# RWKV scan of a two-layer backbone: the substitution issued with its preparation, the group norm later and in another scratch tile, and merged products

## The chip, the cores and the metric

The program runs on one core of a Trainium2 chip. The metric is device time in microseconds (us), the median of several executions. The kernel before took 4250.28 us (three runs, 4240.55 to 4259.92).

The engines have short names: PE is the matrix engine (PEld its weight loads), DVE the vector engine, ACT the scalar engine, POOL the GpSimd engine, and SP the engine whose queue issues the DMAs. Each works through its own list of instructions strictly in order; semaphores tie the lists together.

## The reference, cut to what matters

The model has two layers. Each mixes tokens by four head groups, projects the result with `w_out`, and runs a convolutional feed-forward part. The change lies in one of the groups, RWKV-7, a recurrence over 1280 tokens in each of two directions:

```python
def rwkv_scan(r, w, k, v, a, b, state):
    def step(s_mem, inp):
        rt, wt, kt, vt, at, bt = inp
        sa = jnp.einsum('bhvk,bhk->bhv', s_mem, at)
        s_new = s_mem * wt[:, :, None, :] + sa[..., None] * bt[:, :, None, :] + vt[..., None] * kt[:, :, None, :]
        return s_new, jnp.einsum('bhvk,bhk->bhv', s_new, rt)
...
h, h_c = bidirectional_scan(rwkv_scan, rwkv_scan, ctx_fw, ctx_bw, lat_fw, lat_bw, init)
out = lambda hh, bon, gg: gg * (head_group_norm(from_heads(hh), ng, nb) + from_heads(bon))
```

## The kernel before

**Steps.** The recurrence is cut into ten steps of 128 tokens per direction (both directions in one step, each as two chunks of 64). `rwkv` is a generator; each `yield` hands over to the caller. A step s has four parts:

- `rwkv_prep(s)` loads the step's tiles, makes decays and the scaled products `bk` and `ar` on ACT, DVE and POOL, multiplies them on PE into `G`, and cuts the 16-wide diagonal blocks out of `G` into `NB`.
- `rwkv_inverse(s)` is the substitution: a DVE transpose of `NB` into `LM` (line 555), a POOL copy into `XL`, and 30 small POOL products and sums that invert the triangular blocks. `LM` and `XL` have one buffer each.
- `rwkv_tail(s)` builds the full inverse `XT` from `XL` by three DVE transposes and five groups of small matmuls with ACT copies (`ZC`, `Q`, `XT`) between them.
- `rwkv_chain(s)` is the recurrence: four times (two chunks, two directions) a product with the state `SV`, a copy `U` (line 634), a product with `XT`, a copy `VSA`, and the new state, scaled by `rho` (lines 621 and 644).

In program order a step is: substitution of step s+1, chain of s, group norm where two output tiles have become complete (steps 6 to 9, and step 1 in layer 0), tail of s+1, preparation of s+2. The group norm writes its squares and its result into `gq`, which takes the buffer of `LM`, and stores it by a DMA into `yw` (line 679).

**What runs beside it.** The mLSTM group runs in the same stage: after every second of its pieces (19 in layer 0, 17 in layer 1) the scan is advanced by one step. Matmuls for the modulation vectors (line 993, weights `adaw`) are spread between them. When both are through, the `w_out` weights are loaded in 32 pieces through eight buffers (`wst`, line 1060) and split into two halves `wo` by ACT (line 1035) and DVE (line 1036). `mix_out` then loads the groups' outputs (`yt`, line 1158; `gt`, line 1161), transposes them on PE (line 1166), scales them (`yT`), writes `uh` and `ul` (lines 1177, 1178), and multiplies with `wo` (lines 1042 to 1044).

**What sets the order.** The program text gives priorities. A scheduler puts each engine's instructions into one fixed list when the kernel is built, by its own estimate of when their inputs and buffers are ready. A change in one place can therefore move instructions of unrelated parts in that list. The lists of both layers differ from before only in the stage of the scan and just behind it.

Of the kernel before, what the change touches and what calls it, by code (L numbers as in the profile page):

```python
# [429 lines left out]
def rwkv(K,l,pv,last,p1,p2,p3):  # L430


    nc=K.nc; tt=nc.vector.tensor_tensor
    YF=p1.tile([128,10,4,64],F32,name="YF")
    W2=p1.tile([128,512],F32,name="W2"); nc.gpsimd.memset(W2,0.0)
    for i,(w,o) in enumerate((('rwkv_w2','rwkv_w0'),('rwkv_a2','rwkv_a0'))):
        nc.sync.dma_start(W2[i*64:i*64+32].rearrange("p (d c) -> p d c",d=2),K.a[w][l].rearrange("d p c -> p d c"))
        nc.sync.dma_start(W2[i*64+32:i*64+33],K.a[o][l:l+1].rearrange("o d c -> o (d c)"))
    TWA=p1.tile([128,2,2,128],F32,name="TWA"); nc.gpsimd.memset(TWA,0.0)
    rmask=p1.tile([128,2,128],F32,name="rmask"); nc.sync.dma_start(rmask,K.a['c_rwmask'])  # L440
    xl0=p1.tile([128,32,8],F32,name="xl0"); nc.sync.dma_start(xl0,K.a['c_xl0'])
    smask=p1.tile([128,4*65],F32,name="smask"); nc.gpsimd.memset(smask,1.0); nc.gpsimd.memset(smask.rearrange("p (a b) -> p a b",b=65)[:,:,0:1],0.0)
    kas=p1.tile([128,2,2,2],F32,name="kas")
    for a in range(2):
        r=slice(64,128) if a==0 else slice(0,64); o=slice(0,64) if a==0 else slice(64,128)
        nc.gpsimd.memset(kas[o,a],-0.5)
        nc.vector.tensor_scalar(out=kas[r,a,0],in0=pv['ka'][r],scalar1=0.5,scalar2=None,op0=ALU.mult)
        nc.vector.tensor_scalar(out=kas[r,a,1],in0=pv['ka'][r],scalar1=-0.5,scalar2=1.0,op0=ALU.mult,op1=ALU.add)
    AR=[p1.tile([128,2,2,2,2,2,64],F32,name="AR%d"%i) for i in range(3)]
    for t in AR: nc.gpsimd.memset(t[64:128,:,:,:,0],0.0); nc.gpsimd.memset(t[0:64,:,:,:,1],0.0)  # L450
    XT=[p1.tile([128,2,4,128],F32,name="XT%d"%i) for i in range(2)]
    for t in XT: nc.gpsimd.memset(t,0.0)
    I32=p1.tile([128,32],F32,name="I32"); hm=p1.tile([128,2],F32,name="hm"); PI=p1.tile([128,2,4,32],F32,name="PI")
    for i in range(4): nc.scalar.activation(out=I32[i*32:i*32+32],in_=K.ident[i*32:i*32+32,i*32:i*32+32],func=ACTF.Copy)
    for i in range(2): nc.vector.tensor_reduce(out=hm[:,i:i+1],in_=I32[:,i*16:i*16+16],axis=XS,op=ALU.add)
    for i in range(2): nc.scalar.activation(out=PI[:,i],in_=I32.unsqueeze(1).to_broadcast([128,4,32]),func=ACTF.Copy)
    C=dict(AR=AR,XT=XT,I32=I32,hm=hm,PI=PI,YF=YF,W2=W2,TWA=TWA,rmask=rmask,xl0=xl0,smask=smask,kas=kas,p=p2,p3=p3,l=l,pv=pv,last=last,seen=set())
    NS=10
    st=[rwkv_prep(K,C,0)]
    rwkv_inverse(K,C,st[0]); rwkv_tail(K,C,st[0])  # L460
    st.append(rwkv_prep(K,C,1))
    for s in range(NS):
        yield
        if s+1<NS: rwkv_inverse(K,C,st[s+1])
        rwkv_chain(K,C,st[s],st[s+1] if s+1<NS else None,s)
        if s==1 and not last or s>5:
            a,b={1:(8,9),6:(3,4),7:(2,5),8:(1,6),9:(0,7)}[s]
            sl=slice(a,b+1,b-a)
            group_norm(K,YF[:,sl],K.D['yw'].rearrange("(t p) c -> p t c",p=128)[:,sl],2,p2.tile([128,1056],F32,tag="LM",name="gq")[:,0:512].rearrange("p (a t) -> p a t",t=64),"gnw")
        if s+1<NS: rwkv_tail(K,C,st[s+1])  # L470
        if s+2<NS: st.append(rwkv_prep(K,C,s+2))


def rwkv_prep(K,C,s):
# [41 lines left out]
    ar=C['AR'][s%len(C['AR'])]; bk=p3.tile([128,2,2,2,2,64],F32,tag="BK",name="bk")  # L516
    for a in range(2):
        for ft in range(2): act(out=bk[:,:,ft,:,a],in_=As[:,:,ft].rearrange("p d (c t) -> p d c t",t=64),func=ACTF.Identity,scale=C['kas'][:,a,0,ft:ft+1],bias=C['kas'][:,a,1,ft:ft+1])
        for d in range(2): tt(out=bk[:,d,:,:,a],in0=bk[:,d,:,:,a],in1=v4(rkk[:,d,4-2*a:6-2*a]),op=A.mult)
    G=p.tile([128,2,2,2,2,128],F32,tag="G",name="G",bufs=3); bt=p.tile([128,2,2,2,2,64],F32,tag="BKT",name="bt",bufs=3)  # L520
    NB=p.tile([128,2,4,32],F32,tag="NB",name="NB")
    for d in range(2):
        E,N=Ep[:,d],En[:,d]
        if d==0: Wp,W,Wi=E[:,:,:,0:64],E[:,:,:,1:65],N[:,:,:,1:65]
        else: Wp,W,Wi=N[:,:,:,1:65],N[:,:,:,0:64],E[:,:,:,0:64]
        for q in range(2):
            r=slice(q*64,q*64+64)
            (nc.gpsimd if d==0 else nc.vector).tensor_tensor(out=ar[r,d,:,:,q,0],in0=v4(rkk[r,d,6:8]),in1=Wp[r],op=A.mult)
            tt(out=ar[r,d,:,:,q,1],in0=v4(rkk[r,d,0:2]),in1=W[r],op=A.mult)
        for a in range(2): tt(out=bk[:,d,:,:,a],in0=bk[:,d,:,:,a],in1=Wi,op=A.mult)  # L530
        for c in range(2):
            b=bank()
            for f in range(2): mm(b[:,f*256:f*256+256],bk[:,d,f,c].rearrange("p a t -> p (a t)"),ar[:,d,f,c].rearrange("p q a t -> p (q a t)"),start=True,stop=True)
            tt(out=G[:,d,c].rearrange("p f q t -> p (f q) t"),in0=b.rearrange("p (a t) -> p a t",a=4),in1=C['rmask'][:,d].unsqueeze(1).to_broadcast([128,4,128]),op=A.mult)
        for q in range(2):
            for blk in range(2):
                r=slice(q*64+blk*32,q*64+blk*32+32)
                src=G[r,d,:,:,q,blk*32:blk*32+32].rearrange("p c f t -> p (c f) t")
                if d==0: nc.vector.transpose(out=NB[r,0],in_=src)
                else: act(out=NB[r,1],in_=src,func=ACTF.Copy)  # L540
        b=bank()
        for c in range(2):
            for f in range(2):
                nc.tensor.transpose(b[:,c*256+f*128:c*256+f*128+128],bk[:,d,f,c].rearrange("p a t -> p (a t)"),K.ident)
        act(out=bt[:,d].rearrange("p c f q e -> p (c f q e)"),in_=b,func=ACTF.Copy)
# [3 lines left out]
def rwkv_inverse(K,C,P):  # L549

    nc=K.nc; A=ALU; p=C['p']; NB=P['NB']
    LM=p.tile([128,1056],F32,tag="LM",name="LM"); LD=LM.rearrange("p (b s) -> p b s",b=2)
    X=P['X']=p.tile([128,384],F32,tag="XL",name="XL")
    XD=X.rearrange("p (b s) -> p b s",b=2)[:,:,0:64].rearrange("p b (i j) -> p b i j",j=4); tmp=X[:,256:376].rearrange("p (b i j) -> p b i j",b=2,j=4)
    nc.vector.transpose(out=LM[:,0:1024].rearrange("p (j i) -> p j i",i=32),in_=NB.rearrange("p d u j -> p j (d u)").unsqueeze(2).to_broadcast([128,32,4,8]))
    nc.gpsimd.tensor_copy(out=X[:,0:256].rearrange("p (h i j) -> p h i j",h=2,j=4),in_=C['xl0'].rearrange("p i (h j) -> p h i j",h=2))
    for j in range(15):
        n,m=15-j,j//4+1; t_=tmp[:,:,0:n,0:m]
        nc.gpsimd.tensor_tensor(out=t_,in0=LD[:,:,j*33+1:j*32+16].unsqueeze(3).to_broadcast([128,2,n,m]),in1=XD[:,:,j:j+1,0:m].to_broadcast([128,2,n,m]),op=A.mult)
        nc.gpsimd.tensor_tensor(out=XD[:,:,j+1:16,0:m],in0=XD[:,:,j+1:16,0:m],in1=t_,op=A.add)  # L560
# [53 lines left out]
def rwkv_chain(K,C,P,Pn,s):  # L614
# [3 lines left out]
    rho=p.tile([128,2,2,2],F32,tag="rho",name="rho",bufs=2)  # L618
    for i in range(2):
        if i and not Pn: break  # L620
        for d in range(2): tt(out=rho[:,i,d],in0=io[:,1,d,:,i^d],in1=(Pn if i else P)['io'][:,0,d,:,d if i else 1-d],op=A.mult)
    need_y=not(C['last'] and s<2); YF=C['YF']
    if need_y: y=K.ybank(); yb=[y[:,0:256],y[:,256:512]]
    for i in range(2):
# [40 lines left out]
def group_norm(K,Y,out_y,nt,sqt,tag="gn",pool=None):  # L665

    nc=K.nc
    v=Y[:,0:nt]; h=Y.shape[2]; n=nt*h; th=lambda t: t[:,:n].rearrange("p (t h) -> p t h",h=h)
    q=sqt[:,:n].rearrange("p (t h) d -> p t h d",h=h)
    s,r=[th((pool or K.p_sm).tile([128,n],F32,tag=tag,name="gn_"+i,bufs=2)) for i in "sr"]  # L670
    nc.vector.tensor_reduce(out=s,in_=v,axis=mybir.AxisListType.X,op=ALU.add)
    nc.vector.tensor_scalar(out=s,in0=s,scalar1=1.0/64,scalar2=None,op0=ALU.mult)
    nc.vector.tensor_tensor(out=v,in0=v,in1=s.unsqueeze(3).to_broadcast([128,nt,h,64]),op=ALU.subtract)
    nc.scalar.activation(out=q,in_=v,func=ACTF.Square)
    nc.vector.tensor_reduce(out=r,in_=q,axis=mybir.AxisListType.X,op=ALU.add)
    nc.scalar.activation(out=r,in_=r,func=ACTF.Sqrt,scale=1.0/64,bias=K.eps5)
    nc.vector.reciprocal(out=r,in_=r)
    (nc.gpsimd if nt==2 else nc.vector).tensor_tensor(out=q,in0=v,in1=r.unsqueeze(3).to_broadcast([128,nt,h,64]),op=ALU.mult)
    nc.sync.dma_start(out_y,q.rearrange("p t h d -> p t (h d)"))
# [789 lines left out]
```

## Time and profile before

| what | value |
|---|---|
| median of three runs | 4250.28 us |
| profiled execution | 4248.15 us, span 4246.4 us, granted clock 0.946 of full speed |
| PE busy in the span | 3951.2 us (93%) |
| DVE busy | 2537.2 us (60%) |
| scan stage, layer 0 | 767 to 1185 us of the span |
| scan stage, layer 1 | 2933 to 3360 us of the span |

The profile is of one execution; its rows are added up against its own 4248.15 us, which lies 2.1 us under the median. The stage is where step 0 of the scan begins until the last matmul of its last chain. "Idle before" in a row is the time for which the engine had nothing running, and behind the arrow stands what ended it.

### The profile page before, as it was taken

How to read it: one execution, taken by the hardware profiler on the slowest of the kernel's cores; microseconds unless marked ns; L12 is line 12 of the kernel's file. 1: busy time of each engine (PE TensorE's matmuls, PEld its weight loads, DVE VectorE, ACT ScalarE, POOL GpSimd, SP SyncE). 2: the span in 40 equal slices, each digit the busy share in tenths (PEclk: the TensorE clock that was granted, in tenths of full speed). 3: DMA queues.
4: the chain of work that ended last, by engine and by line, in shares of the span. 5: the costliest groups of instructions: out<-in, count | busy, mean ns of one | idle time of the engine just before them, and what ended most of it. 6: DMA issues, size and time to landing. Idle time of an engine off the chain costs nothing.

```text
span 4246.4 us, 70484 instructions
## 1 busy us (share of the span) xinstructions
PE 3951.2 (93%) x28176; PEld 3225.0 (76%) x28176; DVE 2537.2 (60%) x4756; ACT 1413.6 (33%) x2849; POOL 764.7 (18%) x1538
## 2 busy tenths in 40 slices
PE   5999999799979999999997999997899799999998
PEld 2788887677768888888885678886776678888886
DVE  5755665777669444444448565677767684444447
ACT  4433333554344211111113433344543442212121
POOL 3320023323312000000021221025432220000002
PEclk6999999799989999999998999998898799999999
DMA  4235554344443110111103325554333331111112
GB/s 165 76 96 180 151 156 121 109 149 125 129 147 120 46 40 30 45 40 35 35 30 121 90 87 157 171 162 118 118 115 109 124 111 55 50 40 55 45 50 99
DMA packets 477154, 414.50 MB, mean 98 GB/s; under 512 B 48827, under 2 KB 443284, under 8 KB 474010
## 3 DMA queue, kind: packets, MB, share of 16 engines
q1 hardware_dynamic: 476826, 409.99, 31.1%
q8 instruction: 222, 3.64, 0.3%
q14 instruction: 106, 0.87, 0.1%
HBM read 323.65 MB, written 86.25 MB: 97 GB/s over the span
## 4 chain that ended last, share of the span: by engine, by line
PE 53%; DVE 9%; DMA 4%; issue 2%; ACT 2%; POOL 1%; SPq 1%; DVEq 0%; ACTq 0%; POOLq 0%
PE bank L1043 9%; PE bank L1042 9%; PE bank L1044 9%; PE dbank L1042 6%; PE dbank L1043 6%; PE dbank L1044 6%; DVE bst L1003 1%; DMA xt<-x 1%; DVE facc L1225 1%; PE mbank L993 1%; PE bank L186 1%; DMA adaw<-in_ada_w 1%; PE bank L187 1%; DVE facc L1226 0%; DMA wst<-in_w_out 0%
## 5 line engine op out<-in xcount | busy, mean ns | idle before, releaser
L1042 PE MATMUL dbank<-uh,wh 128*128 128x512 f32 (+1 forms) x2120 | 763.7, 369 | 8.6 <-ACT tmpB L398 5.5
L1043 PE MATMUL dbank<-ul,wh 128*128 128x512 f32 (+1 forms) x2120 | 759.8, 367 | 0.0
L1036 DVE TENSOR_TENSOR wl<-wst,wh 128x1024 fp32r<-128x1024 f32 x146 | 185.9, 1275 | 510.3 <-ACT wh L1035 355.1
L1044 PE MATMUL dbank<-uh,wl 128*128 128x512 f32 (+1 forms) x2120 | 481.5, 367 | 0.0
L1042 PEld LDWEIGHTS dbank<-uh,wh 128*128 128x128 f32 x2120 | 400.6, 189 | 84.0 <-ACT tmpB L398 5.9
L1043 PEld LDWEIGHTS dbank<-ul,wh 128*128 128x128 f32 x2120 | 400.9, 189 | 68.7 <-issue 1.1
L1044 PEld LDWEIGHTS dbank<-uh,wl 128*128 128x128 f32 x2120 | 365.7, 188 | 71.0 <-issue 1.7
L1284 DVE TENSOR_TENSOR facc<-facc,bank 128x512 f32<-128x512 f32 x324 | 221.8, 687 | 205.1 <-PE bank L1044 205.1
L1042 PE MATMUL bank<-uh,wh 128*128 128x512 f32 (+1 forms) x920 | 334.9, 372 | 4.5 <-ACT uh L1030 4.5
L1043 PE MATMUL bank<-ul,wh 128*128 128x512 f32 (+1 forms) x920 | 335.1, 372 | 0.8 <-DVE ul L1031 0.8
L1042 PE MATMUL bank<-wdh,gh 128*128 128x512 f32 x792 | 315.6, 400 | 15.7 <-DVE facc L1298 5.7
L1043 PE MATMUL bank<-wdl,gh 128*128 128x512 f32 x792 | 310.4, 392 | 1.0 <-DVE wdl L1036 1.0
L1253 POOL MEMSET fz<- 128x1 f32 x132 | 7.3, 99 | 1433.4 <-DVE fc L1268 1213.5
L1044 PE MATMUL bank<-wdh,gl 128*128 128x512 f32 x792 | 247.7, 391 | 0.0
L1035 ACT ACTIVATE wh<-wst 128x1024 fp32r<-128x1024 f32 x146 | 154.7, 1060 | 237.5 <-PE dbank L1043 164.5
L1035 ACT ACTIVATE wdh<-wst 128x1024 fp32r<-128x1024 f32 x46 | 48.8, 1062 | 523.7 <-PE bank L1044 431.4
L1044 PE MATMUL bank<-uh,wl 128*128 128x512 f32 (+1 forms) x920 | 211.9, 372 | 0.0
L1042 PEld LDWEIGHTS bank<-uh,wh 128*128 128x128 f32 x920 | 174.1, 190 | 36.1 <-ACT uh L1030 5.6
L1043 PEld LDWEIGHTS bank<-ul,wh 128*128 128x128 f32 x920 | 174.2, 189 | 31.9 <-DVE ul L1031 1.7
L1042 PEld LDWEIGHTS bank<-wdh,gh 128*128 128x128 f32 x792 | 149.7, 189 | 56.9 <-DVE facc L1298 11.0
L1044 PEld LDWEIGHTS bank<-uh,wl 128*128 128x128 f32 x920 | 161.5, 188 | 33.1
L1043 PEld LDWEIGHTS bank<-wdl,gh 128*128 128x128 f32 x792 | 149.7, 189 | 34.6 <-issue 3.2
(490 smaller groups left out, 7856.9 us busy)
## 6 DMA issues: line engine op xcount, KB each, us to landing
wst<-in_ffn_w_up SPq DMA_DIRECT2D x88, 512.0 KB
adaw<-in_ada_w SPq DMA_DIRECT2D x160, 256.0 KB
wst<-in_w_in SPq DMA_DIRECT2D x58, 512.0 KB
wst<-in_ffn_w_down SPq DMA_DIRECT2D x46, 512.0 KB
df<-in_c_F SPq DMA_DIRECT2D x10, 1344.0 KB
xt<-x SPq DMA_DIRECT2D x26, 512.0 KB
df<-in_c_I SPq DMA_DIRECT2D x8, 1344.0 KB
rkk<-wrk SPq DMA_DIRECT2D x10, 1024.0 KB
```

The costliest lines, as they stand in the source:

```text
L186: mm(dst_re,F[:,i],pre(slot),start=True,stop=False); mm(dst_re,F[:,i+1],pim(slot),start=False,stop=True)
L187: mm(dst_im,F[:,i],qim(slot),start=True,stop=False); mm(dst_im,F[:,i+2],qre(slot),start=False,stop=True)
L993: for j in range(2): nc.tensor.matmul(ps[32*j:32*j+2,0:128],k.sc[:,q],w[u][q//2][:,q%2,j*128:j*128+128],start=(q==0),stop=(q==7))
L1003: for h in range(2): nc.vector.bn_stats(out=st[:,h],in_=x[h])
L1035: k.nc.scalar.activation(out=h,in_=st,func=ACTF.Copy)
L1036: k.nc.vector.tensor_tensor(out=lo,in0=st,in1=h,op=ALU.subtract)
L1042: mm(ps,lh,rh,start=(i==0),stop=False)
L1043: mm(ps,lh,rl,start=False,stop=False)
L1044: for i,((lh,ll),(rh,rl)) in enumerate(pairs): mm(ps,ll,rh,start=False,stop=(i==n-1 and more is None))
L1225: for o,i,gg in zip([y[:,h] for h in hs],x,[g[:,h] for h in hs]) if parts else [(y,x,g)]: stt(out=o,in0=i,scalar=m,in1=gg,op0=ALU.subtract ...
L1253: for q in (0,1025,1282): nc.gpsimd.memset(z[:,q:q+1],0.0)
L1284: else: tt(out=d,in0=d,in1=ps,op=ALU.add)
```

## The change

Three things are edited. The substitution of step s+2 is written directly behind that step's preparation, so in the program's order it stands one hand-over to the mLSTM earlier, and the group norm is written after tail, preparation and substitution. The group norm's scratch `gq` takes the buffer of `As` (an input of the preparation) and no longer that of `LM`. In the preparation, pairs of DVE products with 256 elements per partition become one with 512 (lines 519 and 530), and the products for `rho` move from DVE to POOL.

```diff
     st=[rwkv_prep(K,C,0)]
     rwkv_inverse(K,C,st[0]); rwkv_tail(K,C,st[0])
-    st.append(rwkv_prep(K,C,1))
+    st.append(rwkv_prep(K,C,1)); rwkv_inverse(K,C,st[1])
     for s in range(NS):
         yield
-        if s+1<NS: rwkv_inverse(K,C,st[s+1])
         rwkv_chain(K,C,st[s],st[s+1] if s+1<NS else None,s)
+        if s+1<NS: rwkv_tail(K,C,st[s+1])
+        if s+2<NS: st.append(rwkv_prep(K,C,s+2)); rwkv_inverse(K,C,st[s+2])
         if s==1 and not last or s>5:
             a,b={1:(8,9),6:(3,4),7:(2,5),8:(1,6),9:(0,7)}[s]
             sl=slice(a,b+1,b-a)
-            group_norm(K,YF[:,sl],K.D['yw'].rearrange("(t p) c -> p t c",p=128)[:,sl],2,p2.tile([128,1056],F32,tag="LM",name="gq")[:,0:512].rearrange("p (a t) -> p a t",t=64),"gnw")
-        if s+1<NS: rwkv_tail(K,C,st[s+1])
-        if s+2<NS: st.append(rwkv_prep(K,C,s+2))
+            group_norm(K,YF[:,sl],K.D['yw'].rearrange("(t p) c -> p t c",p=128)[:,sl],2,p3.tile([128,8,64],F32,tag="As",name="gq"),"gnw")
...
-        for d in range(2): tt(out=bk[:,d,:,:,a],in0=bk[:,d,:,:,a],in1=v4(rkk[:,d,4-2*a:6-2*a]),op=A.mult)
+        tt(out=bk[:,:,:,:,a].rearrange("p d f c t -> p d (f c) t"),in0=bk[:,:,:,:,a].rearrange("p d f c t -> p d (f c) t"),in1=rkk[:,:,4-2*a:6-2*a].rearrange("p d f (c t) -> p d (f c) t",t=64),op=A.mult)
...
-        for a in range(2): tt(out=bk[:,d,:,:,a],in0=bk[:,d,:,:,a],in1=Wi,op=A.mult)
+        bka=bk[:,d].rearrange("p f c a t -> p (f c) a t"); tt(out=bka,in0=bka,in1=Wi.rearrange("p f c t -> p (f c) t").unsqueeze(2).to_broadcast([128,4,2,64]),op=A.mult)
...
-        for d in range(2): tt(out=rho[:,i,d],in0=io[:,1,d,:,i^d],in1=(Pn if i else P)['io'][:,0,d,:,d if i else 1-d],op=A.mult)
+        for d in range(2): nc.gpsimd.tensor_tensor(out=rho[:,i,d],in0=io[:,1,d,:,i^d],in1=(Pn if i else P)['io'][:,0,d,:,d if i else 1-d],op=A.mult)
```

The scheduler's lists show three places where more than the edited lines moved. Line numbers of the changed kernel are one lower from line 472 on.

The first is DVE in layer 1, around the transpose `LM` of the last substitution (step 9). Before, with `gq` and `LM` in one buffer:

```order
L657 TENSOR_TENSOR YF<-ybank,YF 128x2x64 x4
L671 TENSOR_REDUCE gn_s<-YF 128x8
L579 SCALAR_TENSOR_TENSOR PI<-cbank,hm,I_25746 128x4x16 x2
L672 TENSOR_SCALAR gn_s<-gn_s 128x8
L673 TENSOR_TENSOR YF<-YF,gn_s 128x2x256
L675 TENSOR_REDUCE gn_r<-gq 128x8
```

The transpose stands eleven rows further down (line 555), behind this group norm of step 7. In the changed kernel:

```order
L554 STREAM_TRANSPOSE LM<-NB 128x1024
L643 TENSOR_TENSOR SV<-cbank,rho 64x128 x2
L670 TENSOR_REDUCE gn_s<-mV 128x8
L656 TENSOR_TENSOR YF<-ybank,YF 128x2x64 x4
L578 SCALAR_TENSOR_TENSOR PI<-cbank,hm,I_25706 128x4x16 x2
L671 TENSOR_SCALAR gn_s<-gn_s 128x8
L670 TENSOR_REDUCE gn_s<-YF 128x8
```

The transpose moved ahead of the group norm of step 7, and no longer waits for that norm's store.

The second is ACT at the end of the scan in layer 1, where the halves `wo` of `w_out` are made. Before, in the tail of step 9 (`ZC`, `XT`, `Q`):

```order
L637 ACTIVATE VSA<-cbank 64x128
L1035 ACTIVATE wo_31114<-wst 128x256 x4
L1035 ACTIVATE wo_31116<-wst 128x256 x4
L586 ACTIVATE ZC<-cbank 128x128
L1035 ACTIVATE wo_31118<-wst 128x256 x4
L591 ACTIVATE XT_25743<-cbank 32x8x32 x4
L1035 ACTIVATE wo_31120<-wst 128x256 x3
L599 ACTIVATE Q<-cbank 128x128
L1035 ACTIVATE wo_31120<-wst 128x256
```

In the changed kernel, in the chain of step 9 (`U`, `VSA`):

```order
L609 ACTIVATE XT_25703<-cbank 32x4x32
L633 ACTIVATE U<-cbank 128x128
L636 ACTIVATE VSA<-cbank 64x128
L633 ACTIVATE U<-cbank 128x128
L1034 ACTIVATE wo_31034<-wst 128x256 x4
L1034 ACTIVATE wo_31036<-wst 128x256 x4
L636 ACTIVATE VSA<-cbank 64x128
L1034 ACTIVATE wo_31038<-wst 128x256 x3
L633 ACTIVATE U<-cbank 128x128
L1034 ACTIVATE wo_31038<-wst 128x256
```

All 32 splits moved from the tail of step 9 and the first half of the last chain to behind the second `U` of that chain.

The third is SP behind the scan of layer 1, with the loads `yt` for the first transposes of `mix_out`. Before:

```order
L1158 DMA yt<-yr_110 128x2x256
L1158 DMA yt<-yw_111 128x2x256
L679 DMA ym_108<-gq 128x2x256
L1060 DMA wst<-in_w_out 128x256 x22
L679 DMA yw_111<-gq 128x2x256
L1060 DMA wst<-in_w_out 128x256 x2
L679 DMA yw_111<-gq 128x2x256
L1212 DMA rg<-in_ln_g 128x1024
```

In the changed kernel:

```order
L1059 DMA wst<-in_w_out 128x256 x24
L1211 DMA rg<-in_ln_g 128x1024
L1211 DMA rb<-in_ln_b 128x1024
L1183 DMA xt<-x_116 128x1024 x2
L678 DMA yw_111<-gq 128x2x256
L1157 DMA yt<-ym_108 128x2x256
L1157 DMA yt<-yh_109 128x2x256
L1157 DMA yt<-yr_110 128x2x256
L1157 DMA yt<-yw_111 128x2x256
```

The first `yt` loads moved behind all `w_out` loads and the scan's last store `yw`; the 20 transposes that read them and stood on PE before the last tail's end now stand behind the last chain.

## Rows read from the trace of the kernel before

**Rows 1.** Windows, 767 to 1185 and 2933 to 3360 together: length, busy us of each engine.
```profile
sum 845.00, PE 732.92 PEld 570.00 DVE 602.07 ACT 396.49 POOL 282.02; mean PE 366.46 PEld 285.00 DVE 301.03 ACT 198.25 POOL 141.01
```
**Rows 2.** PE's waits, layer 0, 847 to 1185: us in total, times, longest.
```profile
PE mbank L993 <- DVE NUM L805: 2.0, 1, 2.0
...
PE cbank L585 <- DVE PI L579: 0.4, 1, 0.4
```
**Rows 3.** PE's waits, layer 1, 3014 to 3360.
```profile
PE cbank L605 <- ACT Q L599: 7.6, 3, 6.1
...
PE mbank L961 <- DVE ab L960: 3.5, 3, 2.2
...
PE cbank L585 <- DVE PI L579: 0.7, 1, 0.7
```
**Rows 4.** DVE by source line: count, ns shortest/median/longest, first to last start, forms.
```profile
L519 DVE TENSOR_TENSOR bk<-bk,rkk x80: 379/418/1260, 781.1 to 3230.7; 128x256 f32<-128x256 f32 x80
...
L530 DVE TENSOR_TENSOR bk<-bk,Ep x40: 385/422/1148, 784.5 to 3233.1; 128x256 f32<-128x256 f32 x40
...
L621 DVE TENSOR_TENSOR rho<-io x76: 143/152/991, 787.4 to 3295.1; 128x2 f32<-128x2 f32 x76
...
L1174 DVE TENSOR_TENSOR yT<-yT,gt x27: 671/684/693, 1208.0 to 3435.6; 128x512 f32<-128x512 f32 x27
```
**Rows 5.** POOL's smallest product, 767 to 3390: busy us, mean ns.
```profile
L559 POOL TENSOR_TENSOR XL<-LM,XL 128x8 f32<-128x8 f32 x20 | 4.4, 222 | 1.6
```
**Rows 6.** Timeline: start, us, engine; two DVE products beside one POOL product.
```profile
3230.39 1.59 DVE L519 TENSOR_TENSOR bk<-bk,rkk 128x256 f32<-128x256 f32 x2
...
3230.51 1.19 POOL L778 TENSOR_TENSOR mRU<-mVO,cmbd 8x512 f32<-8x512 f32 x1 [4.81 <-PE mbank L781]
```
**Rows 7.** Source line 555, what ended DVE's idle time; then two rows of PE's timeline.
```profile
  DMA yw<-gq: 6.4, 4
...
3309.74 0.66 PE L635 MATMUL cbank<-U,XT 128*128 128x64 f32 x4 [2.85 <-ACT XT L610]
...
3314.49 2.82 PE L1166 MATMUL dbank<-ident,yt 128*128 128x128 f32 x12
```
**Rows 8.** Timeline, tail of step 9: layer 0, then layer 1.
```profile
1150.63 0.68 DVE L569 STREAM_TRANSPOSE T<-XL 128x128 f32<-128x128 f32 x2
...
1166.40 0.27 ACT L610 ACTIVATE XT<-cbank 32x128 f32<-32x128 f32 x1
...
3323.61 0.69 DVE L569 STREAM_TRANSPOSE T<-XL 128x128 f32<-128x128 f32 x2
...
3343.09 0.27 ACT L610 ACTIVATE XT<-cbank 32x128 f32<-32x128 f32 x1
```
**Rows 9.** Timeline of ACT, layer 1: splits of `w_out` and the last chain.
```profile
3328.06 2.56 ACT L1035 ACTIVATE wo<-wst 128x256 fp32r<-128x256 f32 x8 [2.55 <-DMA ym<-gq]
...
3334.99 0.42 ACT L1035 ACTIVATE wo<-wst 128x256 fp32r<-128x256 f32 x1 [2.39 <-DMA wst<-in_w_out]
...
3342.20 0.26 ACT L634 ACTIVATE U<-cbank 128x128 f32<-128x128 f32 x1
...
3346.27 0.28 ACT L634 ACTIVATE U<-cbank 128x128 f32<-128x128 f32 x1
3347.55 0.76 ACT L1035 ACTIVATE wo<-wst 128x256 fp32r<-128x256 f32 x2 [1.00 <-DMA wst<-in_w_out]
```
**Rows 10.** Timeline, layer 1: the scan's last store, the first product of `mix_out`.
```profile
3365.73 0.38 SPq L679 DMA_DIRECT2D yw<-gq  x1
...
3369.09 0.80 PE L1042 MATMUL bank<-wo,uh 128*128 128x512 f32 x1 [4.26 <-ACT uh L1177]
```
**Rows 11.** Timeline, transposes behind the first `yt` loads, layer 0; scaling and split, layer 1.
```profile
1212.29 1.09 PE L1166 MATMUL dbank<-ident,yt 128*128 128x128 f32 x4 [2.90 <-DMA yt<-ym]
...
3377.34 1.94 ACT L1169 ACTIVATE yT<-dbank,pvm 128x256 f32<-128x256 f32 x4 [2.51 <-POOL ul L1178]
3379.30 1.06 ACT L1177 ACTIVATE uh<-yT 128x1024 fp32r<-128x1024 f32 x1
```

## The prediction

> **What bounds the kernel now.** I read five views in this order: the page, busy time by windows, PE's waits in the two scan stages, DVE's instructions by source line, and the timelines of steps 8 and 9 of the scan with what follows them.
>
> Outside the scan's stages, and the first products behind them, nothing is touched. Inside them PE works 732.9 of 845 us [rows 1]. The change adds and removes no matmul, so even an ideal result could only take from the other 112 us, about 56 per layer. DVE works 602 us of the same 845 and POOL 282 [rows 1]: neither is full, and POOL has the most room.
>
> What PE waits for is read next, from step 2 of the scan on. In layer 0 it waits for DVE on seven lines, from `NUM` with 2.0 us to `PI` with 0.4, together 6.0 us [rows 2]. In layer 1 the first line of all is the copy `Q` of ACT, 7.6 us, of which 6.1 is one wait; DVE is behind six lines, from `ab` with 3.5 to `PI` with 0.7, together 9.5 us [rows 3]. So PE loses 15.5 us to DVE in both layers, and no line names POOL. The substitution, which the change moves, is thus not waited for directly in the middle of the scan. It is waited for at one place in an indirect way: the transpose `LM` sits idle 6.4 us in four cases until the group norm's store has read `gq` out of the same buffer, and behind it PE waits 2.85 us for an `XT` at 3309.74 [rows 7].
>
> **The change part by part.**
>
> *Merged products.* Per step, four pairs of 128x256 products on DVE become four products of 128x512. A product takes 0.418 us (line 519) or 0.422 (line 530), and a 128x512 product of two f32 inputs elsewhere in the kernel 0.684 [rows 4]. A pair saves 2×0.42−0.684 = 0.156 us; 80 pairs in 20 steps save 12.5 us of DVE.
>
> *`rho` to POOL.* 76 products of 0.152 us leave DVE [rows 4]: 11.6 us. POOL's nearest product, 128x8, takes 0.222 us [rows 5], so POOL gets 76×0.222 = 16.9 us, over both stages, on top of 282. In POOL's list they stand behind the substitution that feeds the same step's tail, and so in front of the next one. I cost them at nothing: they need only the decays of two preparations, and the state product that reads them comes a whole tail later. If that cover is gone, all 16.9 us would be late; at best they cost nothing.
>
> *What DVE's relief is worth.* DVE loses 24.1 us of work, 1.2 per step, 4% of its 602. What PE can gain from it is bounded by 0 and by 24.1, if DVE set every step. Of the 15.5 us that PE waits for DVE, 9.2 are for the mLSTM and the modulation (`NUM`, `ab`, `modc`, `S` and the like), which wait for their own chains, and 6.3 for products of the scan. I take half of the scan's 6.3, since half of such a chain's length is copies and transposes that stay: −3 us. Of step 0, whose preparation nothing covers, I count the four pairs in full: 4×0.156×2 layers = −1.2 us.
>
> *Another buffer for `gq`, and the substitution earlier.* The transpose `LM` no longer stands behind the norm's store. The bounds are 0 and the 6.4 us of [rows 7]; I take the one wait that PE saw, −2.9 us. What is late next there is the copy chain of the tail itself. `As`, the new buffer, is an input of a preparation, so the next preparation could wait for the store in its turn; it comes half a step later, and in the last four steps, where the norm runs, there are hardly any preparations left (the last is that of step 9). I cost that at nothing; its upper bound is the same 6.4 us.
>
> *The end of layer 1.* Here the lists move most, though no line of it was edited.
> The 20 transposes of `mix_out` that stood between steps 8 and 9 on PE leave that place. Twelve of them took 2.82 us [rows 7]; all 20 would be 4.7 at that rate. Between 2.8 and 4.7 I take −3.7.
> The tail of step 9 loses its neighbours, the splits of `w_out` on ACT. In layer 1 it lasts from 3323.61 to 3343.36, 19.75 us; in layer 0, where no split stands in it, from 1150.63 to 1166.67, 16.04 [rows 8]. I take the difference, −3.7; the bounds are 0 and −7.6, all of `Q`'s waits [rows 3].
> The last chain pays for it. Now it lasts 17.8 us, from its first `U` at 3342.20 to the end of the stage at 3360.0. The splits took ACT from 3328.06 to 3348.3, 20.3 us with their waits for loads, the longest 2.39 [rows 9]. In the changed list all 32 come behind the second `U`, which is 4.1 us into the chain, and the chain's copies stand between them. The chain then lasts 4.1+20.3 = 24.4 us: +6.6. At best ACT's copies slip through at no cost (0); at worst each of the six copies that follow waits for another late load, 6×2.39 = 14.3 more than the 6.6.
> The loads `yt` now stand behind the last store `yw`. That was issued at 3365.73, 5.7 us behind the stage's end, and the first product of `mix_out` began at 3369.09, 9.1 us behind it [rows 10]. With the loads behind the store, what layer 0 and the later tiles show comes in a row: 2.9 us for the load, 1.09 for four transposes, 1.94 for the scaling, 1.06 for `uh` [rows 11]. 5.7+2.9+1.1+1.9+1.1 = 12.7: +3.6. Bounds 0 (modulation products fill the gap) and +7.
>
> *The sum.* −3 −1.2 −2.9 −3.7 −3.7 +6.6 +3.6 = −4.3 us. The profiled execution took 4248.15 us, so 4243.9; the median of the runs is 2.1 higher, so the forecast is 4246 us.
>
> **A rule against the rows.** In [rows 6] two DVE products of line 519 took 1.59 us together, where two of the median are 0.84; a POOL product of 1.19 us began 0.12 us behind the start of the first. The longest of that line is 1.26 us, three times the median [rows 4]. So POOL's work can hold DVE's. The Trainium skill, "SBUF — State Buffer", section "SBUF: two separate sides", says that the two engines share a pair of ports that one of them locks for its whole instruction, a DVE operation with two inputs from SBUF against a POOL operation that reads SBUF. The trace agrees (1.59 us in place of 0.84). By that rule `rho` on POOL would relieve DVE by less than is counted above, which the third rival prices from rows.
>
> **The rivals.**
>
> *First: DVE sets the steps.* PE's waits name many small releasers, and an engine at 71% that feeds each hop of a chain may delay every hop. Then the whole relief of 24.1 us (step 0's included) falls on the path: −24.1 −2.9 −3.7 −3.7 +6.6 +3.6 = −24.2, so 4226 us. Against it: only 15.5 us of PE's waits end on DVE at all [rows 2, 3], and a good part of DVE's work is done for the mLSTM, which gains nothing here.
>
> *Second, on the slower side: the hand-over to `mix_out` in layer 1.* Place: the last chain on ACT, and SP's queue in front of `yt`. The splits wait for loads that come through eight buffers, and a copy of the chain that stands behind a split waits with it. If each of the six copies behind the second `U` meets a load 2.39 us late [rows 9], the chain lasts 14.3 us more, PE has nothing else there, and if the steps and the tail save nothing the sum is −1.2 −3.7 +6.6 +14.3 +3.6 = +19.6: 4270 us. It decides from the point where eight pieces are not loaded when the second `U` is done. For it: three splits already waited 1.0 to 2.55 us for transfers [rows 9]. Against it: the loads need nothing of the scan and have all of tail 9 to fill the eight buffers.
>
> *Third: POOL holds DVE.* If each `rho` on POOL holds DVE for its 0.222 us, 16.9 of the 24.1 us come back, and 7.2 stay. The gain in the steps falls from 3 to 0.9: 4248 us.
>
> *Fourth: it does not do what it says.* The substitution could stand where it stood, since the scheduler orders lists by its own estimate. The lists say otherwise for step 9; in the middle of the scan PE waits for no substitution, so the move is worth nothing there, which the sum already has.
>
> **How the numbers follow.** What a measurement of this kernel can tell from no change is about 0.5%, 21 us: faster means under 4229, slower over 4271.5. The forecast has a chance of 0.58, the first rival 0.17, the second 0.15, the third 0.10. The forecast's own range takes the bounds of its terms partly together: from −12 (6.4 instead of 2.9, chain at no cost) to +8 (the chain at 14.3 with the tail saved), 4236 to 4258. The range that should hold the time takes in the first rival and most of the second's way: 4225 to 4266. Faster: the first rival and a little of the forecast's lower end, 0.20. Slower: the part of the second rival over 4271, and terms that I have not seen, 0.13. The rest, 0.67, is no change.
>
> **What would show it.** Line 518's and 529's products as 128x512 at about 0.68 us, 80 of them; `rho` on POOL at about 0.22. DVE's busy time in the stages down by some 20 us or more (7 if POOL holds it), and PE's waits for DVE from 15.5 to about 12. No wait of `LM` for a store, and none of 2.85 us in front of chain 8. Splits of `w_out` in the last chain, a chain of some 24 us, a tail of step 9 of some 16, and a gap of about 12.7 us between the stage's end and `mix_out`. The forecast is wrong if steps 2 to 8 become shorter by more than 0.5 us each (first rival), if the last chain passes 30 us (second), or if PE waits for POOL anywhere in the middle of the scan.

## The result: 0.56% slower, and where the time is

The changed kernel took 4273.43 us (seven runs, 4267.71 to 4287.85), the kernel before 4250.28 beside it: ratio 1.0056, 95% interval 1.0035 to 1.0077. The forecast was 4246, in a range that ended at 4266.

The profiled executions (4248.15 and 4275.00 us) are cut at the first matmul of a scan stage and at the first product of `mix_out` behind it:

| stretch | before, us | after, us | difference |
|---|---|---|---|
| ahead of layer 0's stage | 767.4 | 768.3 | +0.9 |
| layer 0: scan stage and hand-over | 466.1 | 488.2 | +22.1 |
| between the stages | 1699.1 | 1700.5 | +1.4 |
| layer 1: until the scan's end | 427.3 | 423.3 | −4.0 |
| layer 1: hand-over to `mix_out` | 9.1 | 19.1 | +10.0 |
| behind it | 877.3 | 873.8 | −3.5 |

So most is lost in layer 0, 22.1 of the 26.8 us between the two spans; for that stage the forecast had no term but DVE's relief. Layer 1 loses 6 us net. The windows of these stretches show in which form (columns: stretch, length, then busy us and instructions of PE, PEld, DVE, ACT, POOL, then granted clock, DMA share, GB/s). Before:

```profile
767.40:1233.50 466.10, 394.64 (x6177) 305.55 (x6177) 325.18 (x831) 216.75 (x583) 144.40 (x385) 0.88 0.42 130
2932.70:3369.10 436.40, 364.98 (x5702) 286.53 (x5702) 306.89 (x770) 204.02 (x565) 141.68 (x379) 0.85 0.38 117
```
After:
```profile
768.30:1256.50 488.20, 403.38 (x6177) 308.48 (x6178) 318.34 (x753) 219.38 (x585) 164.42 (x424) 0.86 0.40 124
2957.00:3399.40 442.40, 371.82 (x5697) 286.64 (x5697) 297.20 (x692) 205.34 (x566) 154.31 (x417) 0.84 0.38 117
```
In layer 0 PE does the same 6177 matmuls. Its idle time (length less busy) goes from 71.5 to 84.8 us, +13.3; and the matmuls themselves take 403.4 us in place of 394.6, +8.7, at a granted clock of 0.86 in place of 0.88 (the clock is granted at one of two levels, full speed or half, and a figure between them is the mean over the stretch). DVE's work did fall, by 6.8 and 9.7 us.

The edited lines look as forecast (count, ns shortest/median/longest; lines of the changed kernel):

```profile
L518 DVE TENSOR_TENSOR bk<-bk,rkk x40: 651/691/1166, 782.0 to 3296.2; 128x512 f32<-128x512 f32 x40
...
L529 DVE TENSOR_TENSOR bk<-bk,Ep x20: 639/684/1062, 784.9 to 3297.9; 128x512 f32<-128x512 f32 x20
...
L620 POOL TENSOR_TENSOR rho<-io x76: 190/368/699, 785.5 to 3317.9; 128x2 f32<-128x2 f32 x76
...
  DVE SV L643: 45.3, 13
```
The merged products are there at 0.69 us. A `rho` on POOL takes 0.368 us, not the 0.222 of [rows 5], and POOL stood idle in front of it 13 times, 45.3 us in all, for the state `SV` of an earlier chain: `rho` has two buffers, and the chain that reads the older one must be through.

PE's waits for DVE did not become fewer. Against [rows 2, 3], the same stretches of after, layer 0 first, then layer 1 (us, times, longest):

```profile
PE cbank L584 <- DVE PI L578: 2.7, 2, 1.7
...
PE cbank L640 <- DVE VSA L636: 2.1, 2, 1.4
```
```profile
PE mbank L960 <- DVE ab L959: 2.9, 3, 2.1
...
PE cbank L584 <- DVE PI L578: 2.2, 2, 1.2
...
PE dbank L543 <- DVE G L533: 1.9, 1, 1.9
```
With the smaller lines they are 8.0 and 11.6 us until the scan's end, 19.6 in place of 16.2 (the prediction's 15.5 left out two small lines, 0.2 and 0.5), though DVE has less to do. PE also waited for POOL, which the prediction had named as a sign of being wrong:

```profile
PE dbank L532 <- POOL rho L620: 0.2, 1, 0.2
...
PE dbank L532 <- POOL AR L527: 0.4, 1, 0.4
```
With 0.6 us in all, these waits are too short to be the loss.

What moved is the mLSTM in layer 0. Its second half runs from the first product `mRU` to the last product `mV` (first and last start in the last two numbers ahead of the forms). Before, then after:

```profile
L781 PE MATMUL mbank<-mRU,mVO x20: 592/592/697, 980.8 to 1185.9; 128*128 128x512 f32 x20
...
L804 PE MATMUL mbank<-mV,S x160: 220/275/417, 1004.8 to 1204.8; 128*128 128x65 f32 x160
```
```profile
L780 PE MATMUL mbank<-mRU,mVO x20: 592/593/1167, 1003.5 to 1208.2; 128*128 128x512 f32 x20
...
L803 PE MATMUL mbank<-mV,S x160: 220/275/477, 1032.2 to 1227.7; 128*128 128x65 f32 x160
```
It lasts 224 us in both, but begins 213.4 us into the stage before and 235.2 after, and ends as much later. In layer 0 it is what ends the stage: the scan's last matmul starts earlier (at 1184.8 before, 1198.5 after), and from the start of the last `mV` to the first product of `mix_out` it is 28.7 us before and 28.8 after. In PE's list 1450 matmuls of the stage stand ahead of its first product before, 1567 after (a trace holds more records than the list has matmuls: 2800 and 3030): a scan step's tail, part of a preparation and half a chain were put in front. No edit speaks of that; the scheduler made the list anew.

### The profile page after: what moved, and what is told of

It is laid out like the page before. It is cut to its first block, busy times and chain, and to the rows that moved or that the text cites. A ratio compares the mean times of both kernels' runs of the same rounds, so it can differ in the third digit from the quotient of the medians.

```text
span 4273.2 us, 70423 instructions
## 1 busy us (share of the span) xinstructions
PE 3970.1 (93%) x28176; PEld 3232.7 (76%) x28176; DVE 2517.1 (59%) x4600; ACT 1415.5 (33%) x2851; POOL 801.7 (19%) x1614
## 4 chain that ended last, share of the span: by engine, by line
PE 70%; DVE 13%; DMA 6%; issue 4%; ACT 3%; POOL 3%; SPq 1%; ACTq 0%; DVEq 0%; POOLq 0%
PE bank L1041 9%; PE bank L1042 9%; PE bank L1043 9%; PE dbank L1041 8%; PE dbank L1042 8%; PE dbank L1043 8%; DMA adaw<-in_ada_w 2%; PE mbank L992 2%; DVE bst L1002 1%; PE bank L187 1%; PE bank L186 1%; PE dbank L532 1%; PE cbank L634 1%; PE cbank L631 1%; PE mbank L780 1%
## 5 line engine op out<-in xcount | busy, mean ns | idle before, releaser
L1041 PEld LDWEIGHTS dbank<-uh,wh 128*128 128x128 f32 x2120 | 401.1, 189 | 84.5 <-ACT tmpB L398 5.8
L1080 ACT ACTIVATE z<-dbank 128x512 f32<-128x512 f32 (+1 forms) x160 | 85.6, 536 | 275.5 <-PE dbank L1043 255.0
```

What stands on the lines that cost most here:

```text
L1041: mm(ps,lh,rh,start=(i==0),stop=False)
L1080: nc.scalar.activation(out=z[:,oo:oo+n],in_=b[:,:n],func=ACTF.Copy)
```

## The experiments

Three theories. L: the remade list of PE costs the time, whatever the edits do. O: the substitution in its new place costs by itself (S: the scan's own steps set the stage; E: any of the edits costs by itself). R: `rho`'s waits on POOL cost. The others are explained where they are used. "Stage" below is layer 0's from its first matmul to the first product of `mix_out`, in the profile. Beside these kernels the kernel before gave medians of 4244.56, 4241.52, 4241.33 and 4244.26 us in the four sets of runs, and each ratio is against the set it belongs to.

**One edit at a time, lists remade.** The edits are lines of the diff shown earlier; for the first:

```diff
-group_norm(..., p2.tile([128,1056],F32,tag="LM",name="gq")[:,0:512]...,"gnw")
+group_norm(..., p3.tile([128,8,64],F32,tag="As",name="gq"),"gnw")
```


> Only the group norm's scratch gq is moved to the buffer of As; program order, products and rho stay as before. Theory L (list): the scheduler's list for PE in layer 0 decides; before, 1450 matmuls of the stage stand ahead of the mLSTM's first product of its second half (line 781), in the changed kernel 1567, and here 1594, so this kernel loses most of what the change lost in layer 0, 12 to 22 us: 4262 to 4272. Theory O (order): the substitution issued with its preparation is what costs; this kernel does not have it: 4245 to 4252. Theory R (rho): rho on POOL costs; not here either: 4245 to 4252.

> Only the pairs of bk products are merged. Theory L: 1540 matmuls stand ahead of the mLSTM's second half in layer 0, so 10 to 20 us lost against 2 to 5 us from DVE's relief: 4255 to 4268. Theories O and R: neither cause is here, and 12.5 us less of DVE give 4240 to 4250.

> Only the rho products move to POOL. Theory R: each group of rho on POOL waits for the state SV of the chain two steps back (45.3 us in 13 waits in the changed kernel) and holds the next work in POOL's queue, so this kernel takes most of the loss: 4262 to 4275, with POOL's wait for SV at 30 to 50 us. Theory O: 4243 to 4251. Theory L: 1594 matmuls ahead of the mLSTM's second half in layer 0: 4260 to 4272, the loss in layer 0 alone, and layer 1 as before within 3 us.

> Program order as in the changed kernel (substitution with its preparation, group norm later, gq in the buffer of As), but unmerged products and rho on DVE. Theory O: the whole loss, 4268 to 4280, layer 0's stage 15 to 22 us longer than before and the hand-over to mix_out in layer 1 some 6 longer. Theory R: 4245 to 4255. Theory L: 1611 matmuls ahead of the mLSTM's second half, so 4265 to 4280 too; what tells L from O is whether the three kernels without the order lose as much in layer 0.

| kernel | median, us | ratio, 95% interval | `mRU` starts, us | stage, us |
|---|---|---|---|---|
| `gq` in `As` alone | 4319.63 | 1.0171 (1.0149 to 1.0194) | 244 | 502 |
| merged products alone | 4255.05 | 1.0023 (1.0010 to 1.0037) | 226 | 480 |
| `rho` on POOL alone | 4280.02 | 1.0075 (1.0058 to 1.0092) | 250 | 502 |
| program order and `gq` | 4266.72 | 1.0052 (1.0032 to 1.0072) | 249 | 495 |

Every edit alone loses, also the one that only takes work off DVE, and the losses do not add up: `rho` alone loses more than all edits together. That speaks for L, but `gq` alone lost more than three times what L expected, and `rho` alone also lost more than expected, so the count of matmuls ahead of `mRU` gives no size. One cost of `gq` by itself is seen. ACT, which writes `As`, sat idle until the norm's store was through: in the changed kernel 4.0 us in two cases (the line below), in `gq` alone 7.6 us in four.

```profile
  DMA yw<-gq: 4.0, 2
```
What these waits cost in the end was not measured.

**The scan handed on earlier or later, and the last `gq` back.** In the first and last of these the scan is advanced one piece of the mLSTM later in layer 0, in the second one piece earlier:

```diff
-                        if i%2: next(scan,None)
+                        if (i%2 if last else i and not i%2): next(scan,None)   # later
+                        if (i%2 if last else not i%2): next(scan,None)         # earlier
```
In the third `gq` goes back to `LM` in step 9 alone:
```diff
-p3.tile([128,8,64],F32,tag="As",name="gq")
+(p2.tile([128,1056],F32,tag="LM",name="gq")[:,0:512]... if s==9 else p3.tile([128,8,64],F32,tag="As",name="gq"))
```


> The changed kernel with one difference: in layer 0 the scan is advanced after pieces 2, 4, 6, ... of the mLSTM in place of 1, 3, 5, ..., so that the scan's work stands one piece later in program order; layer 1 is untouched. Theory L (the list puts the mLSTM's second half late in layer 0, and that half, some 224 us long, sets the stage's end): 1450 matmuls now stand ahead of its first product, as in the kernel before, so that product comes 213 to 220 us into the stage, not 235, the stage of layer 0 up to mix_out is 465 to 473 us, not 488, and the time 4252 to 4260. Theory S (scan: the stage's length comes from the scan's own steps, slower by the substitution's new place): a scan that starts its steps later ends later, 4273 to 4290.

> The kernel before with one difference: in layer 0 the scan is advanced after pieces 0, 2, 4, ... of the mLSTM in place of 1, 3, 5, ..., one piece earlier in program order; nothing of the change is in it. Theory L: 1510 matmuls stand ahead of the mLSTM's second half, not 1450, so it starts 220 to 230 us into the stage and the stage is 473 to 482 us long: 4252 to 4262 in all, though no edit of the change is there. Theory S: the scan's steps come earlier, 4235 to 4250.

> The changed kernel, but the last group norm of the scan (step 9) writes gq into the buffer of LM again; the others stay in that of As. Theory P (pool): the buffer of As lies in the pool that is given up at the scan's end, and mix_out's yt buffers take its room, so in the changed kernel the first yt load waits on SP until the last store of gq is through (3386.92 to 3390.40); here that wait goes, and the time from the last chain matmul to the first product of mix_out in layer 1 falls from 19.1 to 9 to 13 us: 4263 to 4270 in all, layer 0 as in the changed kernel. Rival Q (queue): it is yt's place behind 24 w_out loads and rg, rb and xt on SP that makes it late, whatever buffer gq has: no change, 4270 to 4277, wait for yt 5 us or more.

> Only the merged bk products on the kernel before, and the scan advanced one piece later in layer 0, as in after_late. Theory L: 1450 matmuls ahead of the mLSTM's second half, so layer 0 is as short as before or shorter by what 6 us less of DVE give, 460 to 470 us, and all 4238 to 4250, where the merged products alone gave 4255. Theory S: 4255 to 4270.

The later hand-over made the changed kernel worse: 4292.25 us, 1.0115 (1.0094 to 1.0137), `mRU` at 226 us but a stage of 495. That is a miss for L in the form in which I had put it: with 1450 matmuls ahead of it `mRU` still came later than before, and the second half took 236 us. The merged products with it gave 4254.63, 1.0023 (1.0008 to 1.0037), stage 478: a miss too. The kernel before with the scan earlier, none of the edits in it, lost 21.7 us: 4263.21, 1.0049 (1.0030 to 1.0068); its profile has a stage of 468, 2 us longer than before and not the 473 to 482 that L expected. A changed program order can thus cost without any edit, but where it cost here is not shown; moving the program by hand gives another list with faults of its own, and proves nothing of the edits.

The last `gq` in `LM` settled the hand-over of layer 1. The changed kernel first (start, us, queue or engine):

```profile
3386.92 0.37 SPq L678 DMA_DIRECT2D yw<-gq  x1
3390.40 0.37 SPq L1157 DMA_DIRECT2D yt<-ym  x1
...
3393.25 1.94 PE L1165 MATMUL dbank<-ident,yt 128*128 128x128 f32 x8 [7.24 <-DMA yt<-yh]
...
3399.41 0.80 PE L1041 MATMUL bank<-wo,uh 128*128 128x512 f32 x1 [1.39 <-ACT uh L1176]
```
With the last `gq` in `LM`:
```profile
3367.18 0.42 SPq L1157 DMA_DIRECT2D yt<-ym  x1
...
3382.49 0.36 SPq L678 DMA_DIRECT2D yw<-gq  x1
...
3385.83 0.79 PE L1041 MATMUL bank<-wo,uh 128*128 128x512 f32 x1 [4.90 <-ACT uh L1176]
```
`yt` no longer follows the last store, and the hand-over falls from 19.1 to 9.0 us. That it followed the store was not a matter of place alone; SP's own waits in the changed kernel have this line:

```profile
SPq L1157 <- DMA yw<-gq: 3.0, 1, 3.0
```
The hand-over is 17.8 to 20.4 us in all three kernels in which the last `gq` has the buffer of `As` and the list was remade, 9.0 to 9.8 in the others of the two sets of runs so far. The kernel before on the changed kernel's list of PE, below, has 10.5, so PE's list is not what makes it long. The pool (the stretch of memory that tiles are taken from) in which the buffer lies is closed at the scan's end (`e3.close()`), and a new pool's `yt` takes its room. So P holds for the hand-over. But the median is 4272.84, 1.0065 (1.0046 to 1.0083), in the range that was written for Q: ten us won there were not won in the whole, and the lists had changed once more.

**PE held in a stored list.** To part list from edit, PE's instructions were held in a given order, by dependencies of order alone; the other engines' lists follow. PE has the same matmuls in every version, so either list fits either kernel:

```diff
+    for a,b in zip(o,o[1:]):   # o: the stored order of PE's instructions in both stages
+        tc.add_manual_dep(ins[b],ins[a].name,mybir.DependencyInfo(mybir.DependencyClass.NoSync,mybir.DependencyReason.DATA),reason="hold")
```


> The kernel before, with none of the edits, but PE's instructions held in the order in which they stand in the changed kernel's list (dependencies of order alone, which add no wait; the other engines' lists are made anew around it). Theory L: PE's list is what costs, so it takes most of the change's loss, 4262 to 4278, with layer 0's stage at 478 to 492 us and the mLSTM's second half starting 230 to 240 us into it. Theory E (the edits cost, whatever the list: rho's waits on POOL, the earlier substitution, gq's hold): 4240 to 4252.

> The merged products and rho on POOL, with PE's instructions held in the order of the kernel before. Theory L: nothing is lost, and DVE's 24 us less give 0 to 10 us: 4232 to 4246, layer 0 at 456 to 468 us. Theory E with rho as the cause: 4255 to 4275.

> The changed kernel whole (substitution with its preparation, group norm later, merged products, rho on POOL) but for gq, which stays in the buffer of LM, with PE's instructions held in the order of the kernel before. Theory L: 4232 to 4250, layer 0 at 456 to 470 us, the hand-over to mix_out in layer 1 at 9 to 10 us. Theory E: the order of the substitution or rho still costs, 4258 to 4275.

> The merged products alone, with PE's instructions held in the order of the kernel before (without that hold the merged products gave 4255 us against 4244.6). Theory L: 4236 to 4246, at or below the kernel before; the difference to the run without the hold, 10 us or more, is the list's. Theory E (a longer DVE product holds the work behind it): 4250 to 4258, as without the hold.

With `gq` in `As` the old list would, by the order of its rows, be a deadlock (PE's `yt` transposes stand ahead of the scan's end, and `yt`'s room is free only behind it), so `gq` stays in `LM` in the third; its place with PE held was not tried.

**One layer's list, and one edit, at a time.** The same means; for the first two, one stage's order from the changed kernel and the other's from the kernel before.

> The kernel before, with PE held in the changed kernel's order in layer 0's stage and in its own order in layer 1's. Theory L0 (layer 0's list carries the loss, since the mLSTM's second half begins late there): layer 0 at 482 to 495 us, the whole 4258 to 4275. Theory L1 (it is layer 1's list with its hand-over): 4241 to 4250.

> The kernel before, with PE held in its own order in layer 0's stage and in the changed kernel's order in layer 1's. Theory L0: layer 0 at 464 to 472 us, layer 1 some 5 to 10 longer than before, 4246 to 4256. Theory L1: 4258 to 4275.

> Only rho on POOL, PE held in the order of the kernel before. If rho's waits on POOL for SV (45 us in the changed kernel) delay what stands behind them: 4248 to 4265. If they cost nothing and DVE's 11.6 us less give something: 4230 to 4242, with layer 1 shorter than before by 5 to 15 us, as in the two held runs that had rho on POOL. Without the hold rho on POOL gave 4280 us against 4244.6.

> Only the program order (substitution with its preparation, group norm later), gq in the buffer of LM, PE held in the order of the kernel before. If the earlier substitution is neutral where PE's list stays: 4238 to 4247. If it delays the mLSTM's work on DVE and POOL by itself: 4250 to 4265.

| work of | PE's list of | median, us | ratio, 95% interval | stage, us |
|---|---|---|---|---|
| before | after, both layers | 4288.29 | 1.0118 (1.0089 to 1.0146) | 487 |
| before | after in layer 0 | 4278.80 | 1.0088 (1.0065 to 1.0111) | 500 |
| before | after in layer 1 | 4252.13 | 1.0017 (0.9999 to 1.0035) | 463 |
| after, `gq` in `LM` | before | 4244.71 | 1.0004 (0.9987 to 1.0021) | 471 |
| merged and `rho` | before | 4240.72 | 0.9995 (0.9978 to 1.0011) | 468 |
| merged alone | before | 4253.79 | 1.0016 (1.0004 to 1.0029) | 464 |
| `rho` alone | before | 4245.91 | 1.0003 (0.9986 to 1.0020) | 463 |
| program order alone | before | 4243.01 | 1.0001 (0.9988 to 1.0014) | 476 |

The kernel before, with none of the edits, loses 47 us by the medians with the other list of PE (ratio 1.0118); layer 0's part of that list alone has a ratio of 1.0088, layer 1's 1.0017. The whole change but for `gq`, on the old list, costs nothing that these runs can tell (−6 to +9 us), nor does `rho` alone or the program order alone. So PE's list carries the loss, in both directions of the exchange.

Three things stay open. First, the list costs the kernel before more than the whole change cost (47 us against 23), and in layer 0 more than was expected (a stage of 500 us, not 482 to 495): the list was made for the changed kernel, and how much of the surplus comes from putting it into another was not measured. Second, the merged products alone lose 12.5 us by the medians with the list held and 10.5 without it (4255.05 against 4244.56). That is the range of theory E and a miss for L: for this edit the list is not shown to be the cause. In the profile its two stages are 464.3 and 437.6 us, against 466.1 and 436.4 before, so the loss is not seen in them; with `rho` beside it it is gone, which is not explained. Third, `gq` in the buffer of `As` was never run on the old list.

The list's effect is seen in the same two views. The kernel before on layer 0's list of after:

```profile
767.30:1267.20 499.90, 414.21 (x6178) 316.38 (x6178) 324.90 (x831) 220.19 (x585) 148.90 (x386) 0.84 0.40 121
```
```profile
L781 PE MATMUL mbank<-mRU,mVO x20: 592/593/1167, 1014.1 to 1217.1; 128*128 128x512 f32 x20
```
The whole change but for `gq`, on the list of before:
```profile
771.10:1242.10 471.00, 390.81 (x6177) 301.22 (x6177) 319.70 (x753) 219.82 (x585) 158.44 (x423) 0.89 0.42 128
2939.80:3357.60 417.80, 354.32 (x5701) 279.76 (x5701) 298.73 (x692) 203.37 (x565) 158.08 (x417) 0.88 0.40 122
```
```profile
L780 PE MATMUL mbank<-mRU,mVO x20: 592/593/1057, 983.2 to 1199.0; 128*128 128x512 f32 x20
```
With the other list `mRU` starts 246.8 us into the stage and PE is idle 85.7 us at a clock of 0.84; with the old one it starts at 212.1, idle 80.2, clock 0.89, and the stage is back within 5 us of the kernel before. PE's idle time in the stage tells the two lists apart: it is 71.5 to 80.2 us in the seven kernels on layer 0's list of before, and 84.8 to 88.6 in the three on that of the changed kernel.

`rho`'s waits are in the held kernel as well, and longer than in the changed one:

```profile
L621 POOL TENSOR_TENSOR rho<-io x76: 187/368/1055, 782.1 to 3282.8; 128x2 f32<-128x2 f32 x76
...
  DVE SV L644: 61.4, 14
```
61.4 us of POOL's idle time cost nothing there that the runs can tell (1.0003, −6 to +8 us), so R falls as the cause. The time, 4245.91, lies between the two ranges that were written for this kernel: DVE's 11.6 us less gave nothing either.

## Why the prediction was wrong, step by step

**The step that failed is "The end of layer 1. Here the lists move most".** I priced three places where the rows of the lists had moved, all in layer 1, and for the rest let the lists stand, a term put at nothing without a reason: layer 0 had −2.1 us (its part of DVE's relief and step 0). It measured +22.1. The mLSTM's second half, which ends that stage, had gone back by 117 matmuls; I read the lists for what the scan waits for, not for what the stage ends with. The first rival looked at DVE, the second at the last chain, the third at the ports, the fourth at whether the move took place; none was "the remade list is worse in places that no edit touches". That the loss goes with the old list of PE and comes with the new one is shown; which exchange in the list is at fault is not: in the 18 kernels profiled, the eight with `mRU` at 219 us or sooner have stages of 463 to 476 us, the ten with a later one 478 to 502, but within these the order is loose (226 us went with 480 and with 495).

**The hand-over of layer 1 was mis-sized.** Term +3.6, measured +10.0, outside its bounds of 0 to 7. The loads behind the store were foreseen, but as a matter of SP's row. They waited for the store itself, through a pool that is closed, and `gq`'s new buffer, priced "at nothing" with an upper bound of 6.4 for the next preparation, was the cause; the next preparations waited 4.0 us, within that bound. Step by step from the scan's end (3380.3): the store was issued 6.6 us behind it (5.7 in the sum), the loads 3.5 behind the store (nothing in the sum), the transposes 2.9 behind the loads (2.9), and the first product 6.2 behind the transposes (4.1).

**The scan of layer 1 came out by luck.** −1.5 −0.6 −2.9 −3.7 −3.7 +6.6 = −5.8, measured −4.0, yet not by these parts. The wait of `LM` for a store is gone: what ended DVE's idle time ahead of its line is now ACT alone, against [rows 7].

```profile
  ACT NB L539: 3.7, 5
```
But the tail of step 9 is not 16 us long but 31.0: it began early, at 3330.22, and its first matmul came only at 3351.76, behind chain 8 and beside the mLSTM's last products (the last starts at 3353.0). The last chain is 19.0 us, not 24.4: the splits took less, 15.4 us in place of 20.3, and waited less for loads.

```profile
3330.22 0.69 DVE L568 STREAM_TRANSPOSE T<-XL 128x128 f32<-128x128 f32 x2 [1.58 <-POOL XL L559]
```
```profile
3360.99 0.27 ACT L609 ACTIVATE XT<-cbank 32x128 f32<-32x128 f32 x1
3361.28 0.28 ACT L633 ACTIVATE U<-cbank 128x128 f32<-128x128 f32 x1
...
3365.36 2.56 ACT L1034 ACTIVATE wo<-wst 128x256 fp32r<-128x256 f32 x8 [0.17 <-DMA ym<-gq]
...
3378.89 1.85 ACT L1034 ACTIVATE wo<-wst 128x256 fp32r<-128x256 f32 x5 [0.45 <-DMA wst<-in_w_out]
```
These are the rows of after that answer to [rows 8] and [rows 9]: tail from 3330.22 to 3361.26, chain from 3361.28, splits from 3365.36 to 3380.74.

**DVE's relief.** 24.1 us were counted, and in the pair of profiles DVE's whole busy time fell by 20.1 (2537.2 to 2517.1). One pair decides little here: in the eight profiled kernels in which DVE's work was not edited it lies between 2522.1 and 2541.1, in the five with both edits between 2517.1 and 2527.3. So whether 24 us left DVE or 7, as in the third rival, stays open; the two differ by only 2 us in the time. With both edits on the held list the time changes by −9 to +5 us (0.9978 to 1.0011): that holds the −3, and the first rival, all 24 us on the path, falls.

**`rho` on POOL** at nothing holds, for another reason than the one given. I had written that the products need only two preparations; they also wait for a chain, by their two buffers.

**The range** was added up loosely: the named bounds give −14.4 and +10.0 us, 4236 to 4260, not −12 and +8. Nothing hangs on it.

## What to carry to other kernels

Where a scheduler makes the lists, the price of an edit is that of its work and that of the new list. Here the new list cost up to 47 us and all edits together, but for `gq`, 9 at most. So look for the work that ends each stage, in stages too that no edit touches, and see when it begins; the count of what stands ahead of it is a warning and no price (with 1450 matmuls ahead, the stage took 463 to 495 us). To learn what an edit is worth, hold the bound engine in its old list and time it again; a variant with a remade list tells little of the edit. A scratch tile that is moved to another pool changes who waits when that pool is closed.

## What the runs showed that was not expected

The same list does not give the same stage, because PE's clock differs. The kernel before on the changed kernel's list of PE in layer 0 took 487 us there where it had that kernel's list in layer 1 too (the row below), and 500 where it had not (shown further up), with nearly the same idle time, 88.6 and 85.7 us; the matmuls were busy 398.5 us at a clock of 0.88 and 414.2 at 0.84.

```profile
767.70:1254.80 487.10, 398.51 (x6178) 303.93 (x6178) 325.34 (x831) 220.53 (x585) 150.09 (x386) 0.88 0.41 124
```
Nor does more idle time always come with a lower clock: with the scan one piece earlier the stage had 84.5 us of idle time, as the changed kernel, yet a clock of 0.91 and 383.7 us of matmuls. So of the 22.1 us in layer 0 the list is shown to give the idle time, 13.3 us; that the other 8.7, from the clock, come from it too is not shown.

The clock also moves where no matmul has changed. In the last 100 us ahead of layer 1's stage, before and in the kernel with merged products alone:

```profile
2832.70:2932.70 100.00, 92.02 (x578) 79.21 (x576) 75.24 (x121) 33.69 (x73) 63.91 (x87) 0.93 0.40 119
```
```profile
2864.80:2964.80 100.00, 91.51 (x477) 78.75 (x475) 60.55 (x97) 26.88 (x61) 51.68 (x67) 0.76 0.26 76
```
At 0.76 in place of 0.93 PE got through 477 matmuls, not 578, though it was busy as much, and the stretch between the stages is 1716 us long, not 1699. In 14 profiles it was 1698 to 1705 us long, with 0.91 to 0.97 in these last 100 us; in four it was 1712 to 1716, with 0.76 to 0.78, and nothing lay between. So one profile alone can be some 15 us off, and the medians with their intervals decide here.
